# The low parts of all weights on VectorE, in a two-layer attention trunk

## The chip, the cores and the metric

One core of a Trainium2 chip runs the kernel. The metric is the device time of one execution in microseconds (us), as the median of several runs.

## The reference

The input x has 256 tokens of 1024 features. Two layers follow each other, each with a residual: `x = x + mixer(rms_norm(x))`.

```
layer 0 (nsa):  q, kc, vc, ks, vs, kw, vw, gl, z = split(h @ a_w_in)   # 1024 x 3632
                three causal attentions of 16 heads over 4 key groups:
                compressed keys, selected blocks, window; each with a gate sigmoid(gl)
                y = (gated sum of the three * silu(z)) @ a_w_out        # 1024 x 1024
layer 1 (swa):  q, k, v, z = split(h @ b_w_in)                          # 1024 x 2304
                attention in a window of 128 tokens, 2 key groups, a sink in the softmax
                y = (o * silu(z)) @ b_w_out                             # 1024 x 1024
```

Queries and most keys are normed per head and rotated before they meet. All is float32, and the comparison needs nearly all of its digits.

## The kernel before, in words

[...] To keep the digits, each operand a is split into a rounded part hi(a) and the rest lo(a) = a - hi(a), and a product is the sum hi*hi + hi*lo + lo*hi. So each weight matrix is brought in as tiles of 128 rows by 1024 numbers (two row blocks of 512 columns, four of 256 or eight of 128; three loads are narrower), 63 loads in all, and each tile goes through three steps: a DMA from the queue of SP writes `wraw`, a copy makes the rounded part `wh` (nearly always on ScalarE, L140; a few on VectorE, L142), and a subtraction makes the low part `wl = wraw - wh` (L168 where it is VectorE's, L65 where it is GpSimd's). `wraw`, `wh` and `wl` have five buffers each, so a tile's parts can be made only when TensorE is through with the tile five loads ahead.

Which engine makes a low part is read from the table `WPS` (L38): nine strings, one for each phase of the program (`PHASES`, bounds in loads), and within a phase the letters are taken in turn. `d` is VectorE, `p` is GpSimd, `b` gives the first half of the row blocks to VectorE and the second half to GpSimd. The first load is split in steps of one row block.

The program writes its steps in this order, and a scheduler of the framework, with a timeline of its own, then decides the order of the instructions on every engine; each engine runs its list strictly in order. Layer 0: transposed tokens hT, key and value products (akc, avw, akw, aks), the key preparation (`k_prep`), the compressing network (ph), query products of two groups of eight heads (aq) with `q_prep`, then gates (pz, `z_gate`) and attention (`attend0`: scores s, softmax p, transposes ptp, value products po) for four groups of heads, and the output product (pya, pyb). Layer 1 has the same steps with other names (aqb, akv, sb, pb).

Around the change it is three helpers that matter. `q_prep` and `k_prep` take the products of both halves of the tokens: a sum of squares per head (L307 on ScalarE, L308 on VectorE), the two rotary terms `rt` (L320, L321, VectorE), the reciprocal root `rsqrt` (L244 to L250: one scaling, two integer steps, and three Newton rounds of three small steps each, all on VectorE, on 128 rows of 2 to 16 numbers, in tiles rs_m, rs_t, rs_y), then on GpSimd the addition of the rotary terms and the scaling by the root (both L65, tile `rt`), the rounded part on ScalarE, the low part on VectorE (L260 into `qs`, L373 into `kp`), and transposes of both on TensorE (L347 `ptq`, L376 `ptk`), whose results the scores need. `z_gate` reads a gate's product on VectorE (L391). GpSimd also scales the softmax weights p by their sums (L70).

Of the kernel before, what the change touches and what calls it, by code (L numbers as in the profile page):

```python
"""Two-layer trunk of a hybrid decoder: a sparse-attention mixer, then a sliding-window mixer with sinks.

The sequence has 256 tokens, so the shapes alone decide that the selected branch of the first mixer takes
all four key blocks (NSA_TOPK >= n_blk) and that its window covers every earlier token: both are causal
attention over their own keys and values, and the block scores order a set that is taken whole.

Products run on the tensor engine in float32r passes. An operand a is split exactly into hi(a) + lo(a),
each of 12 mantissa bits, and hi*hi + hi*lo + lo*hi is accumulated in float32.  Queries are stacked as
[hi; lo] against [hi; hi] and [lo; lo] keys, so two passes carry all four products.
"""  # L10
# [19 lines left out]
T = 256  # L30
# [3 lines left out]
EPS = 1e-6  # L34
NEG = -1e30
HP, HPZ, HPS, HPT, HPQ, HPF = 200, 200, 0, 100, 0, 0
RSC, QLO = 'p', 'd'
WPS = ('pbdb', 'bd', 'dppd', 'bd', 'bp', 'p', 'pdp', 'ppd', 'b')  # L38
PHASES = (4, 13, 23, 29, 37, 43, 49, 55)
# [18 lines left out]
class Pool:  # L58
    """GpSimd, with steps by scalars in their two-operation form (a factor of one): its cores run that faster."""

# [18 lines left out]
def swap_halves(ap, n):  # L79
    """[128, n, 64] read with the two 32-wide halves of each head exchanged, as [128, n, 2, 32]."""  # L80
    p, h, d = ap.ap
    return bass.AP(tensor=ap.tensor, offset=ap.offset + 32, ap=[list(p), list(h), [-32, 2], [1, 32]])
# [7 lines left out]
def tile_hybrid_trunk(ctx: ExitStack, tc: tile.TileContext, x, positions, norm_gains, a_w_in, a_cmp_pos,  # L90
# [23 lines left out]

# [1 line left out]
    warm = work.tile([128, 256], BF, name="warm", tag="sq", bufs=1)  # L116
    nc.gpsimd.memset(warm, 0.0)

    def warm_up(n):
        """Products of zeros that keep the tensor engine at its full clock until the first data is there."""  # L120
        pw = bank("pw", "acc")
        for i in range(n):
            mm(pw[:, 0:256], warm[:, 0:128], warm, True, True)
# [6 lines left out]

# [1 line left out]
    nload, NLOW = [0], 4  # L132
# [65 lines left out]
    warm_up(NWARM)  # L198
# [1 line left out]
    ident0 = work.tile([128, 128], F32, name="ident0", tag="rt1")  # L200
# [7 lines left out]
    nc.vector.tensor_copy(gT, pg)  # L208
    # masks to add: [window edge | causal | zero | causal], and those of the compressed keys
    mask = const.tile([128, 512], F32, name="mask")  # L210
# [25 lines left out]

# [1 line left out]
    def rsqrt(dst, src, a, b):  # L238
        """dst = (a * src + b) ** -0.5 by a bit-level guess and three Newton steps."""
        shape = list(src.shape)  # L240
        m = work.tile(shape, F32, name="rs_m", tag="rs_m")
# [10 lines left out]
    def row_rsqrt(dst, s0, s1, a):  # L252
        """dst = (a * (s0 + s1) + EPS) ** -0.5."""
        ss = work.tile(list(dst.shape), F32, name="rs_h", tag="rs_h")
        nc.vector.tensor_tensor(ss, s0, s1, op=ALU.add)
        rsqrt(dst, ss, a, EPS)
# [7 lines left out]
    def norm_transpose(xt, layer, hT, h, ns=(0, 1)):  # L264
        """hT[:, part, k, tokens of half h] = parts of the gain-weighted rows, features on the partitions.

        The norm's factor of each row is left out here; it goes into what is made of the products."""
        for n in ns:
# [14 lines left out]
    def spread(r):  # L283
        """The row factors [tokens, 2] as rows of all partitions, [128, 256]."""
        rows = work.tile([128, T], F32, name="rrows", tag="rrows", bufs=1)
        ones = work.tile([128, 128], F32, name="ones", tag="rt2")
        nc.vector.memset(ones, 1.0)
        pr = ps_t.tile([128, T], F32, name="pr", tag="pt")
        for h in range(2):
            dg = work.tile([128, 128], F32, name="dg", tag="rt1")  # L290
            nc.vector.tensor_scalar(dg, ident, r[:, h:h + 1], None, op0=ALU.mult)
            mm(pr[:, h * 128:(h + 1) * 128], ones, dg, True, True)
        nc.scalar.activation(rows, pr, AF.Copy)
        return rows

    def proj(acc, hT, h, w, nk, k0):
        """acc[tokens of half h, columns] += h @ w over the nk row blocks from k0."""
        wh, wl = w
# [11 lines left out]
    def rope_terms(ps, n, h, tab, eng='d'):  # L310
        """The two terms of the rotated, gain-weighted heads (before the row factor)."""
        t1 = work.tile([128, n, HD], F32, name="rt1", tag="rt1")
# [17 lines left out]
    def q_prep(pss, tab, qTs, h0, rf):  # L330
        """Eight heads of both halves: norm, rotate, split, and stack [hi; lo], head dims on the partitions."""
        ssq = work.tile([128, 2, 8], F32, name="qssq", tag="qssq")
# [17 lines left out]
    def k_prep(pss, ng, tab, kt, c0, rf):  # L350
        """Key heads of both halves: norm, rotate, split, duplicate, transpose into kt[:, part, group, c0[h]:]."""
        ssq = work.tile([128, 2, ng], F32, name="kssq", tag="kssq")
# [26 lines left out]
    def z_gate(hT, wd, c0, zt, g, rows):  # L379
        """zt[:, 2 * g:2 * g + 2, :] = 2 * silu(z) of two column blocks, columns on the partitions."""  # L380
        pz = ps_a.tile([128, 2, T], F32, name="pz", tag="pz")
# [20 lines left out]
    def scores(p, s, mk, floor, nm, total):  # L402
        """p = exp(s + mask - m) with m the larger of the row's maximum and -floor; nm = -m, total = row sum of p."""
        nc.vector.tensor_tensor_reduce(out=p, in0=s, in1=mk, scale=-1.0, scalar=floor, op0=ALU.add, op1=ALU.min,  # L404
# [3 lines left out]
    def finish_unit(po, zt, h, g4, oz):  # L408
        """Gate the four heads 4*g4.. and split them for the output product."""
        if g4 == 3 and h == 1 and 1:  # L410
# [12 lines left out]
    def pv(po, blocks, first):  # L423
        """po += V^T P^T over blocks of (v [keys, 64], four P^T blocks [keys, 4, 128])."""
        for i, (v, ptb) in enumerate(blocks):
# [4 lines left out]
    def transpose_p(srcs):  # L430
        """P^T [keys, 4, 128] from four [128 queries, 128 keys] blocks."""
        pt = ps_t.tile([128, 4, 128], F32, name="ptp", tag="pt")
# [8 lines left out]
    def out_proj(oz, w, xt, sq_out, last):  # L441
        """xt += oz^T w per half; order of row blocks so that half 0 ends early."""
        ws = {}
# [7 lines left out]
        for kk, n, h in order:  # L451
# [9 lines left out]
            if last and h == 1 and n == 1:  # L461
                # the last quarter of the columns has a bank of its own
                for q in range(2):
# [16 lines left out]

    # ================= layer 0 =================
    hT = work.tile([128, 2, 8, T], F32R, name="hT", tag="hT", bufs=1)
# [23 lines left out]

# [1 line left out]
    sinks = const.tile([128, NH], F32, name="sinks")  # L508
# [7 lines left out]
    def rope_tables(cp):  # L516
        """Rows of [-sin, sin, cos] of the angles; the first layer's carry the norm's factor of the row too."""
        trig = cp.tile([128, 2, 3, 32], F32, name="trig")
# [48 lines left out]
    with tc.tile_pool(name="cmp", bufs=1) as cp:  # L567
        w2 = cp.tile([128, HD], F32, name="w2")
        posr = cp.tile([16, 2, 128], F32, name="posr", tag="hr")

        # compressed branch: keys and values of all tokens, two neighbours stacked on the partitions
        ktv = [cp.tile([128, 5, 272], F32, name=f"ktv{i}") for i in range(2)]
# [38 lines left out]
        def keys_selected():  # L611
            # keys and values of the selected and window branches, and the branch gates
            acc = banks("aks", "s")
# [29 lines left out]
        def compress():  # L643
            # the two small networks of the compressed branch
            ph = bank("ph")[:, 0:80].rearrange("p (g c) -> p g c", c=16)
# [12 lines left out]
            nc.vector.scalar_tensor_tensor(hx, hs, 1.0, hx, op0=ALU.add, op1=ALU.mult)  # L658
            # keys
            pk = bank("pk")[0:64, 0:HD]  # L660
# [16 lines left out]
            for part in range(2):  # L677
                nc.vector.tensor_copy(kt[:, part, :, 128:144], pt[:, part].rearrange("p (g c) -> p g c", c=16))
            # values
            hr = cp.tile([128, 4, 4, 16], F32, name="hr", tag="kd")  # L680
# [20 lines left out]
    def attend0(g):  # L701
        for h in range(2):
# [6 lines left out]
            for i in range(4):  # L709
# [21 lines left out]
                for m in range(2):  # L731
                    pm = p[:, m, 0] if h == 0 else p[:, m]
                    scores(pm, svs[m], mks[m], 3e38, nm[:, i, m:m + 1], sums[:, i, m + 1:m + 2])
            # compressed keys, four heads together
            cm = att.tile([128, 4], F32, name="cm", tag="cm")
# [31 lines left out]

    # ================= layer 1 =================
    sqs = work.tile([128, 2, 2], F32, name="sqs1", tag="sqs")
# [113 lines left out]
```

## Time and profile before

| | us |
|---|---|
| median of 3 runs | 316.99 |
| lowest and highest run | 315.06, 317.51 |
| span of the profiled execution | 315.0 |

| engine | busy us | share of the span |
|---|---|---|
| PE (TensorE) | 284.8 | 90% |
| DVE (VectorE) | 238.7 | 76% |
| POOL (GpSimd) | 193.6 | 61% |
| ACT (ScalarE) | 185.9 | 59% |

The profile is of one execution, whose own time outside the span is not listed; the three runs lie 0.03 to 2.5 us above its span. Times in a timeline count from the span's start. An engine's idle time before an instruction is put down to what released it. Where two engines use one resource, the profile shows no wait: an instruction that is held is merely longer.

### The profile page before, as it was taken

How to read it: one execution, taken by the hardware profiler on the slowest of the kernel's cores; microseconds unless marked ns; L12 is line 12 of the kernel's file. 1: busy time of each engine (PE TensorE's matmuls, PEld its weight loads, DVE VectorE, ACT ScalarE, POOL GpSimd, SP SyncE). 2: the span in 40 equal slices, each digit the busy share in tenths (PEclk: the TensorE clock that was granted, in tenths of full speed). 3: DMA queues.
4: the chain of work that ended last, by engine and by line, in shares of the span. 5: the costliest groups of instructions: out<-in, count | busy, mean ns of one | idle time of the engine just before them, and what ended most of it. 6: DMA issues, size and time to landing. Idle time of an engine off the chain costs nothing.

```text
span 315.0 us, 5443 instructions
## 1 busy us (share of the span) xinstructions
PE 284.8 (90%) x1772; PEld 234.5 (74%) x1772; DVE 238.7 (76%) x691; ACT 185.9 (59%) x441; POOL 193.6 (61%) x214
## 2 busy tenths in 40 slices
PE   6979999849999768979999999999929889999995
PEld 4758998637988667856767676889828888787774
DVE  2898359977999996698785433899995999987533
ACT  5674892443435764878888455555228656996610
POOL 6899637951835685563745464539777869583600
PEclk9979999978999995999999999999987979999999
DMA  7969725642454524220020526136724631200003
GB/s 223 319 206 295 286 71 133 208 127 72 128 136 142 182 79 133 69 69 0 2 68 11 193 71 197 21 113 185 211 73 149 198 122 69 67 3 0 1 2 133
DMA packets 33116, 37.53 MB, mean 119 GB/s; under 512 B 1680, under 2 KB 21568, under 8 KB 32960
## 3 DMA queue, kind: packets, MB, share of 16 engines
q1 hardware_dynamic: 33088, 37.18, 38.2%
q8 instruction: 14, 0.23, 0.3%
q14 instruction: 14, 0.11, 0.1%
HBM read 36.13 MB, written 1.05 MB: 118 GB/s over the span
## 4 chain that ended last, share of the span: by engine, by line
PE 40%; DVE 33%; issue 10%; POOL 8%; ACT 3%; DMA 3%; SPq 0%; POOLq 0%; DVEq 0%; ACTq 0%
PE po L113 6%; PE pya L113 6%; PE pz L113 6%; POOL wl L65 5%; PE ptp L434 4%; DVE wl L168 4%; DVE rs_t L248 4%; PE s L113 3%; PE pyb L113 2%; PE akc L113 2%; DVE rs_y L246 2%; PE avw L113 2%; PE aq L113 2%; DMA wraw<-in_a_w_in_dram 2%; DVE rs_m L244 2%
## 5 line engine op out<-in xcount | busy, mean ns | idle before, releaser
L65 POOL TENSOR_TENSOR wl<-wraw,wh 128x1024 fp32r<-128x1024 f32 (+3 forms) x48 | 95.5, 1998 | 33.2 <-ACT wh L140 28.9
L140 ACT ACTIVATE wh<-wraw 128x1024 fp32r<-128x1024 f32 (+3 forms) x58 | 59.3, 1031 | 18.2 <-PE pya L113 3.5
L113 PE MATMUL pz<-hT,wh 128*128 128x256 f32 x256 | 51.4, 296 | 3.3 <-DVE zt L391 3.3
L168 DVE TENSOR_TENSOR wl<-wraw,wh 128x512 fp32r<-128x512 f32 (+3 forms) x38 | 42.1, 1108 | 13.3 <-ACT wh L140 13.2
L113 PEld LDWEIGHTS pz<-hT,wh 128*128 128x128 f32 x256 | 42.5, 201 | 4.5 <-DVE zt L391 3.9
L113 PE MATMUL pz<-hT,wl 128*128 128x256 f32 x128 | 37.8, 295 | 0.0
L70 POOL TENSOR_SCALAR p<-p,rg 128x256 f32<-128x256 f32 (+1 forms) x48 | 21.9, 478 | 21.7 <-DVE rg L742 17.8
L406 ACT ACTIVATE p<-p,nm 128x128 f32<-128x128 f32 (+1 forms) x64 | 28.5, 448 | 6.7 <-DVE nm L404 6.3
L140 ACT ACTIVATE ptsb<-ptp 128x512 f32<-128x512 f32 x36 | 20.8, 591 | 12.0 <-PE ptp L434 11.9
L65 POOL TENSOR_TENSOR rt<-rt,rt 128x512 f32<-128x512 f32 (+2 forms) x14 | 16.4, 1175 | 16.9 <-DVE rt L321 13.0
L404 DVE CUSTOM_DVE_ANT_0 p<-s,mask 128x128 f32<-128x128 f32 (+1 forms) x64 | 21.1, 347 | 6.5 <-PE s L113 5.9
L113 PEld LDWEIGHTS pz<-hT,wl 128*128 128x128 f32 x128 | 25.6, 200 | 0.1
L113 PE MATMUL s<-kt,qT 128*128 128x272 f32 (+1 forms) x96 | 21.7, 318 | 2.4 <-DVE nm L404 2.4
L113 PE MATMUL aqb<-wh,hT 128*128 128x512 f32 x64 | 22.0, 416 | 0.0
L113 PE MATMUL aq<-wh,hT 128*128 128x512 f32 x64 | 21.5, 408 | 0.0
L113 PEld LDWEIGHTS s<-kt,qT 128*128 128x128 f32 x96 | 14.9, 192 | 7.4 <-issue 2.1
L70 POOL TENSOR_SCALAR pb<-pb,rg 128x128 f32<-128x128 f32 (+1 forms) x24 | 11.7, 504 | 11.6 <-DVE rg L838 4.5
L406 ACT ACTIVATE pb<-pb,nm 128x128 f32<-128x128 f32 (+1 forms) x32 | 14.2, 445 | 5.4 <-DVE nm L404 5.1
L347 PE MATMUL ptq<-identr,qs 128*128 128x128 f32 x64 | 8.2, 272 | 9.2 <-DVE qs L260 8.9
L434 PE MATMUL ptp<-identr,p 128*128 128x128 f32 x96 | 15.9, 279 | 0.0
L113 PE MATMUL po<-ptsb,vv 128*64 128x256 f32 x96 | 15.4, 403 | 0.0
L347 PEld LDWEIGHTS ptq<-identr,qs 128*128 128x128 f32 x64 | 7.2, 154 | 10.9 <-DVE qs L260 9.5
(248 smaller groups left out, 762.4 us busy)
## 6 DMA issues: line engine op xcount, KB each, us to landing
wraw<-in_a_w_in_dram SPq DMA_DIRECT2D x25, 512.0 KB, 3.9
wraw<-in_b_w_in_dram SPq DMA_DIRECT2D x18, 512.0 KB, 3.9
wraw<-in_a_w_out_dram SPq DMA_DIRECT2D x8, 512.0 KB, 3.8
wraw<-in_b_w_out_dram SPq DMA_DIRECT2D x8, 512.0 KB, 4.0
x<-in_x_dram SPq DMA_DIRECT2D x4, 256.0 KB, 4.2
w<-in_cmp_w_dram SPq DMA_DIRECT2D x1, 1024.0 KB, 5.3
x<-in_x_dram SPq DMA_DIRECT2D x2, 512.0 KB, 3.7
wraw<-in_a_w_in_dram SPq DMA_DIRECT2D x2, 456.0 KB, 3.8
```

What stands on the lines that cost most here:

```text
L65: self.eng.tensor_tensor(out, a, b, op=op)
L70: self.eng.tensor_scalar(out, a, s0, s1, op0=op0, op1=op1)
L113: nc.tensor.matmul(o, lhsT=l, rhs=r, start=start, stop=stop)
L140: nc.scalar.activation(dst, src, AF.Copy)
L168: e_.tensor_tensor(wl[:, ks], raw[:, ks], wh[:, ks].bitcast(F32), op=ALU.subtract)
L244: nc.vector.tensor_scalar(m, src, a, b, op0=ALU.mult, op1=ALU.add)
L246: nc.vector.tensor_scalar(y.bitcast(I32), t.bitcast(I32), -1.0, 1597463007.0, op0=ALU.mult, op1=ALU.add)
L248: nc.vector.tensor_tensor(t, y, y, op=ALU.mult)
L347: nc.tensor.transpose(pt[:, i], qs[:, 4 * b + i].rearrange("p a d -> p (a d)"), identr)
L404: nc.vector.tensor_tensor_reduce(out=p, in0=s, in1=mk, scale=-1.0, scalar=floor, op0=ALU.add, op1=ALU.min, accum_out=nm)
L406: nc.scalar.activation(p, p, AF.Exp, scale=-1.0, bias=nm, accum_out=total)
L434: nc.tensor.transpose(pt[:, i], s, ident)
```

## The change

The table `WPS` gives every low part to VectorE. Since all letters are `d`, a tile's low part is one instruction, and of the first load, which goes in steps, two. Nothing else of the program differs: the rest of the difference takes out comments and docstrings line by line, so that the line numbers stay.

```diff
-WPS = ('pbdb', 'bd', 'dppd', 'bd', 'bp', 'p', 'pdp', 'ppd', 'b')
+WPS = ('d', 'd', 'd', 'd', 'd', 'd', 'd', 'd', 'd')
```

The scheduler then writes other orders on every engine. First place, TensorE, where the second group of queries of layer 0 is transposed (ptq); before:

```order
L113 MATMUL pz<-hT,wl 128x256
L113 MATMUL s_1311<-kt,qT_192 128x256 x2
L347 MATMUL ptq<-identr,qs 128x128 x8
L113 MATMUL s_1319<-kt,qT_192 128x272 x2
L347 MATMUL ptq<-identr,qs 128x128 x4
L113 MATMUL pz<-hT,wh 128x256 x2
```

And now, where pz is a gate's product and s a score's:

```order
L113 MATMUL pz<-hT,wl 128x256
L113 MATMUL s_1221<-kt,qT_191 128x272 x2
L113 MATMUL s_1230<-kt,qT_191 128x272 x2
L347 MATMUL ptq<-identr,qs 128x128 x8
L113 MATMUL s_1288<-kt,qT_192 128x272 x2
L113 MATMUL s_1292<-kt,qT_192 128x256 x2
L347 MATMUL ptq<-identr,qs 128x128 x8
L113 MATMUL s_1300<-kt,qT_192 128x272 x2
```

Before, 48 of the 192 products pz of layer 0 stand behind this ptq; now the last of them stands ahead of it, and eight more of the score products stand behind it. VectorE's list has 23 instructions for low parts ahead of the second qs that this ptq reads before, and 35 now.

Second place, TensorE in layer 1, the first ptq there, between the products of the second query group (aqb); before:

```order
L113 MATMUL aqb_2897<-wh,hT_2374 128x512 x2
L113 MATMUL aqb_2897<-wl,hT_2374 128x512
L113 MATMUL aqb_2897<-wh,hT_2374 128x512
L347 MATMUL ptq<-identr,qs 128x128 x8
L113 MATMUL aqb_2898<-wh,hT_2374 128x512
```

And now:

```order
L113 MATMUL aqb_2884<-wl,hT_2360 128x512
L113 MATMUL aqb_2884<-wh,hT_2360 128x512
L113 MATMUL pz<-hT_2360,wh 128x256 x2
L113 MATMUL pz<-hT_2360,wl 128x256
...
L347 MATMUL ptq<-identr,qs 128x128 x8
L113 MATMUL pz<-hT_2360,wl 128x256
```

Before, 30 of the 48 products aqb of the second group stand ahead of the ptq and 18 behind it; now all 48 and 11 products of the second gate stand ahead.

Third place, VectorE in layer 1, where the reciprocal roots of the first query group (128x16) begin; before:

```order
L244 TENSOR_SCALAR rs_m<-qssq 128x16
L168 TENSOR_TENSOR wl<-wraw,wh 128x1024
L245 TENSOR_SCALAR rs_t<-rs_m 128x16
L308 TENSOR_REDUCE kssq<-sq 128x2
L246 TENSOR_SCALAR rs_y<-rs_t 128x16
L248 TENSOR_TENSOR rs_t<-rs_y 128x16
L249 SCALAR_TENSOR_TENSOR rs_t<-rs_t,rs_m 128x16
```

And now:

```order
L168 TENSOR_TENSOR wl<-wraw,wh 128x1024 x2
L244 TENSOR_SCALAR rs_m<-qssq 128x16
L308 TENSOR_REDUCE kssq<-sq 128x2
L168 TENSOR_TENSOR wl<-wraw,wh 128x1024
L245 TENSOR_SCALAR rs_t<-rs_m 128x16
L168 TENSOR_TENSOR wl<-wraw,wh 128x1024
L308 TENSOR_REDUCE kssq<-sq 128x2
L246 TENSOR_SCALAR rs_y<-rs_t 128x16
L391 TENSOR_TENSOR zt_2449<-pz,rrows 128x512
```

The low parts that stood in GpSimd's list now stand between the small steps: from layer 1's first residual addition (L477) to the second qs there are 13 in VectorE's list, where there were 3.

## Rows read from the trace of the kernel before

**Rows 1.** The page: span; engine, busy us, share of the span, instructions.

```profile
span 315.0 us, 5443 instructions
PE 284.8 (90%) x1772; PEld 234.5 (74%) x1772; DVE 238.7 (76%) x691; ACT 185.9 (59%) x441; POOL 193.6 (61%) x214
```

**Rows 2.** Timeline of PE: start, duration, instruction, in brackets the idle time before it.

```profile
68.23 0.72 PE L376 MATMUL ptk<-identr,kp 128*128 128x128 f32 x4 [4.26 <-POOL rt L65]
...
118.81 1.25 PE L347 MATMUL ptq<-identr,qs 128*128 128x128 f32 x8 [3.40 <-DVE qs L260]
...
235.71 1.26 PE L347 MATMUL ptq<-identr,qs 128*128 128x128 f32 x8 [5.53 <-DVE qs L260]
...
253.41 0.50 PE L113 MATMUL pz<-hT,wh 128*128 128x256 f32 x2 [2.02 <-DVE zt L391]
```

**Rows 3.** A stretch: length, busy PE, PEld, DVE, ACT, POOL (instructions), granted clock, DMA share, GB/s.

```profile
66.70:73.50 6.80, 5.27 (x36) 4.53 (x37) 4.58 (x14) 4.18 (x8) 3.51 (x5) 0.50 0.55 148
```

**Rows 4.** Groups by form: count, busy us, mean ns, idle before.

```profile
L65 POOL TENSOR_TENSOR wl<-wraw,wh 128x1024 fp32r<-128x1024 f32 x24 | 59.0, 2468 | 10.7 <-ACT wh L140 10.7
L65 POOL TENSOR_TENSOR wl<-wraw,wh 128x512 fp32r<-128x512 f32 x22 | 34.1, 1552 | 22.5 <-ACT wh L140 18.2 <-DVE wh L142 2.4 <-DMA wraw<-in_a_w_in_dram 1.9
L168 DVE TENSOR_TENSOR wl<-wraw,wh 128x1024 fp32r<-128x1024 f32 x15 | 22.3, 1489 | 4.3 <-ACT wh L140 4.3
```

**Rows 5.** Timeline of DVE in 217 to 236 us.

```profile
219.47 1.21 DVE L168 TENSOR_TENSOR wl<-wraw,wh 128x1024 fp32r<-128x1024 f32 x1
...
223.16 2.32 DVE L248 TENSOR_TENSOR rs_t<-rs_y 128x16 f32<-128x16 f32 x1
225.52 0.18 DVE L249 SCALAR_TENSOR_TENSOR rs_t<-rs_t,rs_m 128x16 f32<-128x16 f32 x1
...
228.48 0.97 DVE L249 SCALAR_TENSOR_TENSOR rs_t<-rs_t,rs_m 128x4 f32<-128x4 f32 x1
...
231.80 2.26 DVE L248 TENSOR_TENSOR rs_t<-rs_y 128x4 f32<-128x4 f32 x1
```

**Rows 6.** Timeline of POOL in 217 to 236 us.

```profile
223.04 2.41 POOL L65 TENSOR_TENSOR wl<-wraw,wh 128x1024 fp32r<-128x1024 f32 x1
227.37 2.06 POOL L65 TENSOR_TENSOR rt<-rt,qr 128x512 f32<-128x512 f32 x2 [1.92 <-DVE rs_t L249]
229.39 4.65 POOL L65 TENSOR_TENSOR wl<-wraw,wh 128x1024 fp32r<-128x1024 f32 x2
```

**Rows 7.** Timeline of DVE in 45 to 119 us: first and last of eight held steps.

```profile
46.78 2.36 DVE L244 TENSOR_SCALAR rs_m<-kssq 128x8 f32<-128x8 f32 x1
...
109.39 2.05 DVE L248 TENSOR_TENSOR rs_t<-rs_y 128x16 f32<-128x16 f32 x1
```

**Rows 8.** Tile wl alone: stage, length, busy PE, PEld, DVE, POOL, clock, DMA.

```profile
0.00:45.00 45.00, 19.35 (x54) 11.22 (x54) 10.92 (x12) 11.73 (x9) 0.96 0.75 245
45.00:119.00 74.00, 30.81 (x90) 17.36 (x90) 12.61 (x12) 24.25 (x12) 0.95 0.44 128
119.00:193.00 74.00, 15.16 (x42) 8.52 (x42) 2.16 (x3) 20.77 (x10) 0.96 0.25 77
193.00:236.00 43.00, 21.63 (x65) 12.15 (x64) 4.50 (x2) 19.95 (x8) 0.98 0.44 126
```

**Rows 9.** Busy time of all instructions by stage (columns as in Rows 3).

```profile
0.00:45.00 45.00, 40.22 (x214) 34.06 (x215) 27.98 (x70) 29.77 (x51) 32.62 (x57) 0.96 0.75 245
45.00:119.00 74.00, 62.83 (x415) 53.85 (x413) 68.45 (x164) 35.42 (x70) 48.20 (x38) 0.95 0.44 128
119.00:193.00 74.00, 71.41 (x446) 52.94 (x446) 46.08 (x217) 53.70 (x160) 42.53 (x56) 0.96 0.25 77
193.00:236.00 43.00, 37.48 (x224) 32.32 (x223) 39.27 (x83) 19.27 (x34) 26.97 (x16) 0.98 0.44 126
```

**Rows 10.** The chain of waits in 262 to 268 us: start, duration, piece.

```profile
264.19 2.89 PE pz L113 x22
```

**Rows 11.** Waits: who waited for whom, us in total, times, longest.

```profile
DVE wl L168 <- ACT wh L140: 13.2, 12, 2.6
```

## The prediction

> **What bounds the kernel now.** I read the page's busy shares first, then TensorE's waits in order of time, then the two vector engines beside each other in the stages around those waits. TensorE is busy 284.8 of 315.0 us; VectorE 238.7 and GpSimd 193.6 [rows 1]. So the time is TensorE's work plus what it stands still. It stands longest at four places: 4.26 us at 64 us, 3.40 at 115, 5.53 at 230 and 2.02 at 251 [rows 2], 15.2 us in all, and each time a chain of small steps on VectorE, or a row scaling on GpSimd that waits for one, ends last. [...]
>
> The chains are long because VectorE is held. A low part of 128x1024 on GpSimd takes 2468 ns, on VectorE 1489 [rows 4]. What the reader is to see in [rows 5, 6] is what the two cost each other: from 229.39 us GpSimd has two low parts, 4.65 us, and in that time VectorE's step on 128x4 numbers at 231.80 takes 2.26 us and ends with the second of them. The same kind of step takes 0.18 us at 225.52, when GpSimd is idle. At 223.16 it is 2.32 us beside one low part of 2.41 us.
>
> **The change, part by part.** It does what it says: the built order has no low part on GpSimd and 64 instructions for it on VectorE (38 now, the halves of a shared tile becoming one).
>
> *What is added to VectorE.* Undisturbed, a 128x1024 costs it 1.21 us [rows 5]; of 128x512 I take half of that and a little, 0.69 us. GpSimd's 48 pieces are 24 of 1024 and 22 of 512 numbers a row [rows 4] and two narrower ones, together some 36 tiles of 1024: 36 x 1.21 = 43.6 us more. GpSimd loses 24 x 2.468 + 22 x 1.552 + 2.6 for the two = 95.9 us.
>
> *What VectorE gets back.* In 45 to 119 us eight of its steps are held by a low part of GpSimd, the first at 46.78 us (2.36 us for 128x8), the last at 109.39 us (2.05 us) [rows 7]; against 0.18 us each, or 1.21 for a low part of its own, they lose 12.5 us. GpSimd's low parts there fill 24.25 us [rows 8]: 7 of 1024 and 4 of 512 and the start of a twelfth, which cost VectorE 7 x 1.21 + 4 x 0.69 = 11.2 us. In 193 to 236 us six held steps lose 12.2 us ([rows 5] has two of them), and 8 pieces of 1024 (19.95 us on GpSimd) come to 9.7 us. So in both stages in which VectorE is nearly full (68.45 of 74 us, 39.27 of 43 [rows 9]) its load stays what it is, within 3 us. In the other stages it has room, and those pieces are hidden: 46.08 busy of 74 us between 119 and 193 us [rows 9]. If that cover were gone, the 20.77 us of GpSimd there would come to 20.77 x 1.21 / 2.47 = 10.2 us.
>
> *What is moved in the order.* The scheduler puts more of TensorE's work ahead of the transposes it waits for. First place, second query group: all 192 products of the gates (pz) stand ahead of the waiting ptq, where 48 stood behind it; 8 score products stand behind that were ahead. From 22 pz in 2.89 us [rows 10], 0.131 us each: 48 x 0.131 = 6.3 us, less 8 x 0.14 = 1.1: 5.2 us of the stop is filled, if VectorE comes to its second qs when it does now. Does it? By then it has done 35 low parts, not 23: 35 x 1.21 less 1.6 for the narrower ones is 40.7 us, 17.2 more than the 10.92 + 12.61 now spent [rows 8]. Of these, half of GpSimd's 11.73 us ahead of 45 us (5.9) falls where VectorE is idle 17 us [rows 9]; 12.5 us and some 2.5 of the first stage come back. Each low part of VectorE now waits 13.2 / 38 = 0.35 us on average for ScalarE's rounded part [rows 11], and behind it waits all of VectorE's queue; 12 more make 4.2. 17.2 - 5.9 - 15 + 4.2 = +0.5 us. Term: -4.7 us.
>
> Second place, layer 1: 18 more products of aqb and 11 of pz stand ahead of the ptq that waits 5.53 us. 11 x 0.131 = 1.4; an aqb has twice the columns, so 18 x 0.26 = 4.7: 6.1 us. VectorE's load there is even, but ten more low parts stand ahead of qs and wait 0.35 each: +3.5. Term: -2.6 us.
>
> Against it, the 48 pz are missing where they stood, beside the first softmax groups. TensorE is busy 71.41 of 74 us there [rows 9]; without filler it can stand still between 0 and 6.3 us more. No row lies near either end: VectorE, on which the scores wait, has 28 us of room in that stage, but the first groups now start just behind its full stage. I take half, +3 us.
>
> The sum is -4.7 - 2.6 + 3 = -4.3 us: the span goes from 315.0 to 310.7. The median of the runs shown, 316.99, lies 1.96 us above the profiled span (the runs go from 315.06 to 317.51), and I carry that over: **312.7 us**. The first term lies between -11 (GpSimd's row scalings, no longer behind 2.4 us pieces, bring qs 6 us earlier) and +3 (half the relief fails); the second between -5.5 and +3.5; the third between 0 and +6.3. [...]
>
> The row shows that the hold lasts until GpSimd's piece ends. [...]
>
> **The rivals.**
> 1. *VectorE becomes the bound (slower).* It is in order: a low part whose rounded part or buffer isn't there stops the reciprocal roots, scores and splits behind it. For it: in two stages it is over 90% busy, and GpSimd's row scalings, which stay, also hold it (0.97 us at 228.48 beside the scalings from 227.37 [rows 5, 6]). If half the relief fails, the first term is -4.7 + 7.5 = +2.8, the second -2.6 + 6.1 = +3.5, with +3 from the third: +9.3, or **326 us**. It decides when more than 4.3 of the 27.2 us of both reliefs fails, a sixth. Against it: the holds are seen to end with GpSimd's low parts. Chance 0.34. [...]
> 2. *The stops only move (no change).* TensorE's work is the same, and the missing filler costs its full 6.3 us: -4.7 - 2.6 + 6.3 = -1.0, **316 us**. For it: the softmax groups hang on VectorE and ScalarE both. Against it: VectorE's room in that stage [rows 9]. Chance 0.24.
> 3. *The stops vanish (much faster).* All 15.2 us go but 5, and half of what a slow stretch costs (1.7) with them: 317.0 - 11.9 = **305 us**. For it: every one of them ends on a held chain. Against it: the pieces come into the same queue. Chance 0.08.
>
> The forecast has 0.34. A measurement of this kernel tells 1% from no change, 3.2 us: faster means below 313.8, slower above 320.2. Faster is the forecast and rival 3, 0.42; within 1% 0.24; slower 0.34. The likeliest case's own range is 308 to 316; the range that reaches over most of the others is 304 to 326.
>
> **What would show it.** In the profile after: no low part on GpSimd, and its busy time near 193.6 - 95.9 = 98 us; VectorE between 240 and 262 us; its small steps of the roots at 0.2 us, hardly any above 1; low parts of 128x1024 at 1.2 us. TensorE's stop before the second ptq under 2 us, and that of layer 1 under 3. If VectorE's waits for ScalarE's rounded parts grow well past 25 us, or TensorE stands before the first softmax groups for more than 6 us, rival 1 or 2 has it. The forecast is wrong if the small steps stay long without GpSimd's low parts, for then something else holds them.

## The result, and the profile after

The changed kernel takes 304.44 us (median of four runs, 303.87 to 306.27) against 316.13 us (four runs, 315.06 to 317.51): a ratio of 0.9637, 95% interval 0.959 to 0.9685. It is 3.6% faster, where 1.4% was forecast, and 304.44 is just inside the range.

First the page of the kernel after, as [rows 1]: span; then engine, busy us, share, instructions.

```profile
span 302.5 us, 5413 instructions
PE 284.7 (94%) x1772; PEld 232.3 (77%) x1772; DVE 231.9 (77%) x717; ACT 186.1 (62%) x441; POOL 110.2 (36%) x166
```

TensorE's work is the same to 0.1 us. What is gone is its standing still: the idle times in its timeline add up to 26.6 us before and to 14.2 after, 12.4 of the 12.5 us that the span lost. VectorE has 26 low parts more and is busy 6.8 us less.

The timeline of PE after, its transposes and longest stops, in answer to [rows 2] (start, duration, instruction, idle time before it):

```profile
69.50 0.54 PE L376 MATMUL ptk<-identr,kp 128*128 128x128 f32 x4
...
103.89 0.88 PE L347 MATMUL ptq<-identr,qs 128*128 128x128 f32 x8 [1.83 <-DVE qs L260]
...
114.63 0.89 PE L347 MATMUL ptq<-identr,qs 128*128 128x128 f32 x8 [0.32 <-DVE qs L260]
...
119.03 0.76 PE L113 MATMUL s<-kt,qT 128*128 128x272 f32 x4 [1.25 <-DVE nm L404]
...
229.66 0.80 PE L347 MATMUL ptq<-identr,qs 128*128 128x128 f32 x8
...
237.92 0.50 PE L113 MATMUL pz<-hT,wh 128*128 128x256 f32 x2 [1.95 <-DVE zt L391]
```

The 4.26 us at the ptk (the fourth group of four, now at 69.50) and the 5.53 us at layer 1's ptq have gone altogether. The ptq that waited 3.40 us, that of the second query group, waits 0.32 (at 114.63). A new stop of 1.83 us stands ahead of the first group's ptq (at 103.89), which waited for nothing before. The pz stop stayed (2.02, now 1.95).

Two stretches after (length, busy PE, PEld, DVE, ACT, POOL with instructions, granted clock, DMA share, GB/s), the first over the place of [rows 3], the second beside the first softmax groups:

```profile
60.00:89.00 29.00, 29.00 (x216) 24.63 (x215) 22.63 (x49) 15.19 (x27) 12.88 (x12) 1.00 0.49 133
...
120.00:130.50 10.50, 9.74 (x38) 7.38 (x40) 6.91 (x48) 7.71 (x31) 3.49 (x9) 0.51 0.13 46
```

In the first TensorE never stands (busy 29.00 of 29.00 us) and its granted clock is 1.00. In the second the granted clock is 0.51: of 10.5 us some 5.1 are lost, by an estimate from that clock, behind the stops at 114 to 119 us.

Groups by form after, as [rows 4] (count, busy us, mean ns, idle before):

```profile
L168 DVE TENSOR_TENSOR wl<-wraw,wh 128x1024 fp32r<-128x1024 f32 x59 | 77.1, 1312 | 17.8 <-ACT wh L140 17.5
...
L65 POOL TENSOR_TENSOR rt<-rt,rt 128x512 f32<-128x512 f32 x8 | 13.8, 1728 | 16.8 <-DVE qr L250 6.1 <-PE akv L113 4.6 <-DVE rt L321 4.5
...
L248 DVE TENSOR_TENSOR rs_t<-rs_y 128x16 f32<-128x16 f32 x12 | 2.6, 217 | 0.1
...
L244 DVE TENSOR_SCALAR rs_m<-qssq 128x16 f32<-128x16 f32 x4 | 0.7, 170 | 0.0
```

The same forms before, which [rows 4] did not show:

```profile
L65 POOL TENSOR_TENSOR rt<-rt,rt 128x512 f32<-128x512 f32 x8 | 12.2, 1535 | 10.3 <-DVE rt L321 8.5 <-DVE rs_t L245 1.4 <-DVE rs_m L244 0.5
...
L248 DVE TENSOR_TENSOR rs_t<-rs_y 128x16 f32<-128x16 f32 x12 | 6.6, 548 | 0.2
...
L244 DVE TENSOR_SCALAR rs_m<-qssq 128x16 f32<-128x16 f32 x4 | 4.4, 1106 | 0.0
```

The small steps have their short time back, most of them (1106 to 170 ns, 548 to 217), and GpSimd's row additions are longer (1535 to 1728 ns). VectorE's timeline after, in 210 to 230 us, answers to [rows 5]: between low parts the small steps take 0.16 us, and the one of 1.00 us stands beside GpSimd's row scalings.

```profile
218.25 0.16 DVE L246 TENSOR_SCALAR rs_y<-rs_t 128x16 int32<-128x16 int32 x1
...
219.08 1.21 DVE L168 TENSOR_TENSOR wl<-wraw,wh 128x1024 fp32r<-128x1024 f32 x1
220.22 0.16 DVE L245 TENSOR_SCALAR rs_t<-rs_m 128x4 int32<-128x4 int32 x1
...
225.82 1.00 DVE L250 SCALAR_TENSOR_TENSOR kr<-rs_t,rs_y 128x4 f32<-128x4 f32 x1
```

### The profile page after: what moved, and what is told of

Same layout as the page of the kernel before. It is cut to its first block, busy times and chain, and to the rows that moved or that the text cites. A ratio compares the mean times of both kernels' runs of the same rounds, so it can differ in the third digit from the quotient of the medians.

```text
span 302.5 us, 5413 instructions
## 1 busy us (share of the span) xinstructions
PE 284.7 (94%) x1772; PEld 232.3 (77%) x1772; DVE 231.9 (77%) x717; ACT 186.1 (62%) x441; POOL 110.2 (36%) x166
## 4 chain that ended last, share of the span: by engine, by line
PE 74%; DVE 15%; issue 3%; POOL 2%; DMA 2%; ACT 2%; SPq 1%; ACTq 0%; DVEq 0%
PE po L113 9%; PE pz L113 8%; PE pya L113 8%; PE aq L113 7%; PE pyb L113 7%; PE ptp L434 6%; PE aqb L113 5%; DVE wl L168 5%; PE s L113 5%; PE aks L113 4%; PE avw L113 2%; DMA posi<-in_positions_dram 2%; PE akw L113 2%; PE akv L113 2%; PE ph L113 2%
## 5 line engine op out<-in xcount | busy, mean ns | idle before, releaser
L168 DVE TENSOR_TENSOR wl<-wraw,wh 128x1024 fp32r<-128x1024 f32 (+2 forms) x64 | 81.9, 1285 | 19.1 <-ACT wh L140 18.8
L113 PE MATMUL pz<-hT,wh 128*128 128x256 f32 x256 | 50.4, 294 | 2.8 <-DVE zt L391 1.9
L113 PEld LDWEIGHTS pz<-hT,wh 128*128 128x128 f32 x256 | 42.1, 199 | 3.5 <-DVE zt L391 2.1
L65 POOL TENSOR_TENSOR rt<-rt,rt 128x512 f32<-128x512 f32 (+2 forms) x14 | 22.2, 1588 | 30.1 <-DVE rt L321 16.6
L113 PEld LDWEIGHTS s<-kt,qT 128*128 128x128 f32 x96 | 16.5, 216 | 6.9 <-issue 3.1
L113 PE MATMUL aqb<-wh,hT 128*128 128x512 f32 x64 | 20.6, 394 | 0.0
L113 PE MATMUL aq<-wh,hT 128*128 128x512 f32 x64 | 20.5, 394 | 0.0
L434 PE MATMUL ptp<-identr,p 128*128 128x128 f32 x96 | 16.9, 291 | 0.0
L404 DVE CUSTOM_DVE_ANT_0 pb<-sb,mask,nsink 128x128 f32<-128x128 f32 (+1 forms) x32 | 11.8, 411 | 5.4 <-PE ptp L434 4.0
L434 PEld LDWEIGHTS ptp<-identr,p 128*128 128x128 f32 x96 | 11.7, 147 | 3.9 <-issue 1.8
L65 POOL TENSOR_TENSOR rt<-rt,qr 128x512 f32<-128x512 f32 x8 | 10.2, 1295 | 11.9 <-DVE rs_t L248 9.3
L406 ACT ACTIVATE pb<-pb,nm 128x128 f32<-128x128 f32 (+1 forms) x32 | 14.2, 444 | 0.6 <-DVE nm L404 0.6
```

What stands on the lines that cost most here:

```text
L65: self.eng.tensor_tensor(out, a, b, op=op)
L113: nc.tensor.matmul(o, lhsT=l, rhs=r, start=start, stop=stop)
L168: e_.tensor_tensor(wl[:, ks], raw[:, ks], wh[:, ks].bitcast(F32), op=ALU.subtract)
L406: nc.scalar.activation(p, p, AF.Exp, scale=-1.0, bias=nm, accum_out=total)
L434: nc.tensor.transpose(pt[:, i], s, ident)
```

## Experiments

Two things changed at once: the place of the low parts, and with it the order that the scheduler gives TensorE. TensorE's traced instructions are the same 1643 in both kernels, so either order can be laid on either kernel by edges that fix the order of issue alone.

For each kernel two starts on TensorE serve as milestones: that of the last product of layer 0's output (pyb), and that of the last product of all (tail). Here are the two of the kernel after, from its timeline; before they stand at 199.59 and 311.22 us.

```profile
194.51 0.39 PE L113 MATMUL pyb<-wh,oz 128*128 128x512 f32 x1
...
299.05 0.28 PE L113 MATMUL tail<-wh,ozb 128*128 128x256 f32 x1
```

The first milestone is called layer 0 below, the difference of the two layer 1. Each comes from one profiled execution, so a difference under 1 us says little.

| kernel | low parts | order | time, us | ratio (95%) | layer 0 | layer 1 |
|---|---|---|---|---|---|---|
| before | shared | old | 316.1 | 1 | 199.59 | 111.63 |
| x1 | VectorE | old | 311.7 | 0.9843 (0.9797-0.989) | 199.03 | 106.01 |
| x2 | shared | new | 321.9 | 1.0147 (1.0101-1.0192) | 201.16 | 117.31 |
| after | VectorE | new | 304.4 | 0.9637 (0.959-0.9685) | 194.51 | 104.54 |
| x9 | VectorE | old, then new | 309.7 | 0.9814 (0.9735-0.9893) | 199.28 | 105.23 |
| x10 | VectorE | new, then old | 307.0 | 0.9693 (0.9612-0.9773) | 195.65 | 106.59 |

### Place and order apart: x1 and x2

```diff
+ORDER = {'EngineType.PE': '0-21 30 36 31-33 37-39 ...'}   # x1: the order of before
+def pin_order(nc, tc):
+    ...
+        for a, b in zip(idx, idx[1:]):
+            tc.add_manual_dep(traced[b], traced[a].name, mybir.DependencyInfo(
+                mybir.DependencyClass.NoSync, mybir.DependencyReason.DATA), reason="order")
...
         tile_hybrid_trunk(tc, *args, out)
+        pin_order(nc, tc)
```

x1 is this on the changed kernel. 

> All low parts on VectorE, but TensorE's instructions in exactly the order of the kernel before (issue order alone; ScalarE's follows to within a place or so). Theory A (the holds: VectorE's small steps no longer wait for GpSimd's low parts): the gain stays, 302 to 308 us, and TensorE's stop at the first ptk, 4.26 us before, is below 1. Theory B (the new order of TensorE's work fills the stops): the gain goes, 313 to 318 us. Theory C (GpSimd's row additions and scalings no longer queue behind its low parts): as A.

x2 is the kernel before with the order of after. 

> The low parts shared as before, TensorE's instructions in exactly the order of the changed kernel. Theory B: 303 to 308 us, the stops filled. Theories A and C: 312 to 322 us, with the stops at ptk and ptq still 3 us and longer; work put ahead of a late ptq can win at most what my prediction gave it, 7 us.

x1 lies between the ranges of A and B. x2 lies just inside A's (321.9 us), but its stops at the ptk and at layer 1's ptq are 2.65, 1.85 and 2.38 us, under the 3 that A gave them, and TensorE stands ahead of gate products instead. So neither theory holds alone: the new place alone gains 1.6%, the new order alone loses 1.5%, and together they gain 3.6%. The order pays only with the new place. The stops of x1, as [rows 2]:

```profile
60.35 0.75 PE L376 MATMUL ptk<-identr,kp 128*128 128x128 f32 x4 [2.47 <-ACT kp L367]
...
67.92 0.54 PE L376 MATMUL ptk<-identr,kp 128*128 128x128 f32 x4
...
119.97 0.37 PE L347 MATMUL ptq<-identr,qs 128*128 128x128 f32 x1 [4.51 <-DVE qs L260]
...
232.19 0.88 PE L347 MATMUL ptq<-identr,qs 128*128 128x128 f32 x8 [2.58 <-DVE qs L260]
```

In the old order the second ptq waits longer than before (4.51 against 3.40), layer 1's ptq half as long (2.58 against 5.53). The ptk that waited 4.26 us waits for nothing in x1 (at 67.92), but now the first of the four groups waits 2.47, at 60.35, where it waited 0.54. So place alone gave layer 0 nothing (199.03 against 199.59) and layer 1 5.6 us. The stage of the ptk, 40 to 100 us, in before, x1 and after (length, busy PE, PEld, DVE, ACT, POOL with instructions, granted clock, DMA share, GB/s):

```profile
40.00:100.00 60.00, 54.01 (x343) 45.56 (x340) 51.53 (x106) 27.23 (x46) 34.61 (x25) 0.94 0.45 126
```

```profile
40.00:100.00 60.00, 53.67 (x332) 44.95 (x331) 47.90 (x114) 28.76 (x48) 18.01 (x17) 0.92 0.51 141
```

```profile
40.00:100.00 60.00, 59.12 (x404) 51.78 (x402) 48.61 (x113) 29.91 (x46) 19.20 (x18) 1.00 0.55 158
```

TensorE stands still for 6.0 us of them before, 6.3 in x1 and 0.9 after: here the new place alone only moves the stops, and the order on top of it fills them. The two longest stops in x2:

```profile
107.05 0.76 PE L113 MATMUL pz<-hT,wh 128*128 128x256 f32 x2 [5.72 <-DVE rs_t L249]
...
256.47 0.79 PE L113 MATMUL pz<-hT,wh 128*128 128x256 f32 x2 [4.99 <-DVE zt L391]
```

With GpSimd's low parts still there, gate products that were put ahead wait 5 us for VectorE in both layers: the new order runs TensorE close behind VectorE's list. In the changed kernel the nearest such stops are 0.88 us (at 95.31) and 1.95.

### Which layer: x8, x9, x10

x8 takes the change in layer 0 alone.

```diff
-WPS = ('pbdb', 'bd', 'dppd', 'bd', 'bp', 'p', 'pdp', 'ppd', 'b')
+WPS = ('d', 'd', 'd', 'd', 'd', 'p', 'pdp', 'ppd', 'b')
```

> Low parts all on VectorE in layer 0 (loads 0 to 36), shared as before in layer 1. In the trace of the changed kernel the end of layer 0's output product comes 5.1 us earlier, that of the kernel 12.5. If the two layers' gains add, 310 to 313 us; if layer 0's gain is lost again, 315 to 318 us.

311.8 us, ratio 0.9866 (0.9796 to 0.9936); layer 0 at 194.88, layer 1 111.56 long. The gains of the layers add, and neither is lost again.

x9 and x10 lay the old order on one layer of the changed kernel (the list of x1 cut at its 993rd instruction, the end of layer 0's output product; the other layer keeps the new order).

```diff
+        idx = [i for i in idx if i < 993]   # x9; x10: i >= 993
```

> All low parts on VectorE; TensorE's instructions in the order of the kernel before up to the end of layer 0's output product, in the order of the changed kernel from there. With the old order throughout the time was 311.7 us, with the new one 304.4. Theory D (layer 0's order carries the difference, mostly the products put ahead of the ptk and beside the gates, which my prediction gave no term): 309 to 312 us. Theory E (my terms: the first place with its missing filler is worth 1.7 us, the second 2.6): 305 to 307 us.

> As the last, the other way round: the order of the changed kernel in layer 0, that of the kernel before in layer 1. Theory D: 304 to 306 us. Theory E: 306 to 308 us, with 1 to 3 us of stop at layer 1's first ptq.

In the new place the order is worth 4.8 us in layer 0 (199.28 against 194.51) and 2.1 in layer 1 (106.59 against 104.54). x9's time is in theory D's range, x10's in E's: D holds for the larger part, and layer 1's part is near the forecast's term.

### The place of the second ptq: x13

The 48 products of layer 0's last gate go back behind the ptq of the second query group; all else is the changed kernel. The place in TensorE's list:

```diff
-s x4, pz x16, ptq x4, pz x32, s x4, ptq x8, s x4, ptq x8, s x16, ptcs, ptp x4
+s x4, ptq x4, s x4, ptq x8, s x4, ptq x4, pz x19, ptq x4, s x12, pz x6, s x4, ptcs, pz x14, ptp x4, pz x9
```

> The changed kernel with its own order on TensorE but for the 48 products of layer 0's last gate (pz), which stand where they stood before the change: behind the second group's first ptq and beside the first softmax groups. My prediction's first and third terms together (-4.7 + 3) make their new place worth 1.7 us: then 305 to 307 us. If their absence beside the softmax groups costs more than they fill (7.3 us of stop and half clock are lost there in the trace of the changed kernel), 299 to 303 us.

305.57 us, ratio 0.9654 (0.9609 to 0.9699); layer 0 ends at 195.39, 0.9 us later than after. Its stops there:

```profile
109.73 1.29 PE L113 MATMUL s<-kt,qT 128*128 128x272 f32 x4 [2.40 <-DVE nm L404]
...
112.42 1.25 PE L347 MATMUL ptq<-identr,qs 128*128 128x128 f32 x8 [1.40 <-DVE qs L260]
```

The two more stops take what the filler gives back behind them. The net of the first and third term, 1.7 us, is compatible with that, and so is nothing at all, since the interval overlaps that of the changed kernel. That the missing filler costs more than its products fill (299 to 303 us) is not.

### Hold or queue: x3 to x6, x14

That VectorE is held is read in the timeline; but GpSimd's own row steps also queued behind its low parts, and the change frees both. x3, x4 and x5 put work back on GpSimd in the changed kernel, in its fixed order, for the old share of tiles (the pattern is the old WPS). The line of x3, x4 and x5:

```diff
+scr = wpool.tile(list(raw.shape), BF, name="scr", tag="scr", bufs=1)
+pool.tensor_tensor(scr[:, ks], raw[:, ks], wh[:, ks].bitcast(F32), op=ALU.subtract)          # x3
+pool.tensor_scalar(scr[:, ks], wh[:, ks].bitcast(F32), 1.0, 1.0, op0=ALU.mult, op1=ALU.mult)  # x4, twice
+pool.memset(scr[:, ks], 0.0)                   # x5, three times, behind a scaling of 128x16 of wh
```

> The changed kernel with its order on TensorE fixed; GpSimd in addition does the subtraction of its old share of tiles into a scratch tile (bf16) that nobody reads, so its load and its two-input steps are back and nothing waits for their result. Theory A: the small steps of the roots are again 1 to 2.4 us beside them, VectorE's load grows by 20 to 35 us, and the time is 314 to 328 us. Theory B: 303 to 306 us. Theory C: 310 to 317 us.

> As the kernel with the extra subtractions, but each is replaced by two GpSimd steps that scale the rounded part by one (one input, the same scratch tile), near 1.05 us each for 128x1024 by the step of that size in the trace of before, so about 70 to 85 us of GpSimd's time are filled. In the trace of before, steps with one input on GpSimd hardly lengthen VectorE's. Theory A: 303 to 308 us, small steps at 0.2 us. Theory C: GpSimd's row steps queue behind them as before the change, 310 to 317 us. Theory B: 303 to 306 us.

> As the kernel with one-input extras, but each extra is three GpSimd steps that only write (memsets of the scratch tile) behind a scaling of 128x16. GpSimd's queue is filled again; the extras read next to nothing. Theory A (holds), if a memset holds nobody: small steps at 0.2 us and 303 to 309 us. Theory C (GpSimd's own row steps queue behind such pieces): 310 to 325 us even with small steps at 0.2 us. If memsets hold VectorE as well, the small steps show it and the run tells nothing between A and C.

They took 350.8, 332.5 and 323.4 us (ratios 1.1091, 1.0487, 1.0257). x3 is longer than any theory had it: VectorE, with all low parts and the holds, is busy 283.9 us, 52 more than in the changed kernel. x4 and x5 were meant as controls that hold nobody, and are not. From x5: the group of the memsets, VectorE's steps with one input in 209 to 213 us, the memsets of that time, and a product with two inputs beside other memsets (L253, L254 and L257 are L244, L245 and L248 of before):

```profile
L74 POOL MEMSET scr<- 128x1024 bf16 x72 | 69.8, 970 | 3.0
...
209.59 0.95 DVE L253 TENSOR_SCALAR rs_m<-rs_h 128x2 f32<-128x2 f32 x1
...
210.57 0.97 DVE L254 TENSOR_SCALAR rs_t<-rs_m 128x2 int32<-128x2 int32 x1
...
209.56 2.97 POOL L74 MEMSET scr<- 128x1024 bf16 x3
...
231.12 0.18 DVE L257 TENSOR_TENSOR rs_t<-rs_y 128x16 f32<-128x16 f32 x1
...
230.10 2.97 POOL L74 MEMSET scr<- 128x1024 bf16 x3
```

Beside memsets, whose mean is 0.97 us, these two steps with one input took 0.95 and 0.97 us, the product with two inputs 0.18. So x5 alone tells nothing between A and C, as its expectation allowed. The three together tell something. TensorE's order is the same in them, and GpSimd's queue does not get shorter from one to the next (it is busy 214.3, 222.3 and 231.8 us), while VectorE's busy time falls (283.9, 263.4 and 237.1 us) and the time falls by 27 us. So work on GpSimd that holds VectorE more costs more, though its queue is no longer. On the other side, x5 takes 19 us more than the changed kernel with VectorE busy only 5 us more. That points at the queue, but does not show it, since the memsets' holds lie on the same chains.

x6 and x14 go the other way: the shared low parts stay, and GpSimd's row steps move to VectorE; in x14 TensorE has the old order in addition.

```diff
-RSC, QLO = 'p', 'd'
+RSC, QLO = 'd', 'd'
-RSK, KLO = 'p', 'dp'
+RSK, KLO = 'd', 'dp'
-OZL, RTE, SSE = 'd', 'p', 'd'
+OZL, RTE, SSE = 'd', 'd', 'd'
```

> The kernel before, low parts shared as before, but the row additions and row scalings of queries and keys on VectorE instead of GpSimd, so that nothing on the way to a transpose queues behind GpSimd's low parts. Theory C: 305 to 312 us. Theory A: the holds stay (small steps to 2.3 us) and VectorE gets about 15 us more to do: 313 to 322 us.

> The kernel before, low parts shared as before, row additions and scalings of queries and keys on VectorE, TensorE's instructions exactly in the old order. Layer 1 (from the end of layer 0's output product to the last product) takes 111.5 us in the trace of before and 105.9 with the low parts on VectorE in the same order. Theory C (queue): 105 to 108. Theory A (holds): 110 to 113, with steps of 2.3 us still there. Whole time: C 309 to 313, A 314 to 318 us.

x6: 312.6 us, ratio 0.9897 (0.9853 to 0.994), between the two theories. x14: 322.5 us, ratio 1.0158 (1.0099 to 1.0217); layer 1 takes 115.97 us, 4.3 more than before. Theory A had that direction, though not the size, and the holds go on in x14. From the timelines of VectorE and TensorE there:

```profile
225.87 2.32 DVE L246 TENSOR_SCALAR rs_y<-rs_t 128x16 int32<-128x16 int32 x1
...
232.74 2.36 DVE L249 SCALAR_TENSOR_TENSOR rs_t<-rs_t,rs_m 128x4 f32<-128x4 f32 x1
...
232.87 0.88 PE L347 MATMUL ptq<-identr,qs 128*128 128x128 f32 x8 [1.02 <-DVE qs L260]
```

But at layer 1's first ptq x14 gains more than x1: the stop of 5.53 us is 1.02 there and 2.58 in x1, and from the second sum of squares to qs VectorE takes 14.47 us (217.66 to 232.13), against 18.97 before and 15.45 in x1. What x14 loses stands behind it, at a ptk (2.18 us), a pz (2.53) and a ptp that waits for a scaling on GpSimd (3.26). Its row steps are also shorter, and VectorE's own list differs. So how x1's gain is shared between the end of the holds and the shorter queue stays open: no run takes the holds away and leaves GpSimd's load.

### Further on VectorE: x7, x12, x11, x15

x7 makes the edit of x6 in the changed kernel. x12 makes it for RSC and RSK alone. x11 is x7 with one scaling more on VectorE.

```diff
-PSL = 'pppd'
+PSL = 'dpdd'   # x11
```

> The changed kernel with the row additions and scalings on VectorE too. They are the two-input steps on GpSimd that still hold VectorE (8 to 9 of the 15 us that its steps lose there beside their undisturbed time), and each is near 1 us shorter on VectorE. Theory A: the time falls on, to 297 to 303 us. Rival (VectorE becomes the bound, 232 us busy and some 15 more): 306 to 312 us.

> The changed kernel with the row scalings alone on VectorE, the row additions still on GpSimd. Theory A: half of the remaining holds by GpSimd's row steps go (3.9 us of VectorE's excess is beside the scalings), 301 to 305 us. If the time is set by TensorE's work and what stops remain elsewhere, 304 to 306 us.

> The changed kernel with the row additions and scalings on VectorE and, in layer 1, one of GpSimd's three scalings of probabilities of a head group (of four) moved to VectorE as well (two on each). TensorE's longest stop in the kernel with the rows on VectorE, 3.58 us at 255.85 us, waits for such a scaling on GpSimd. If that stop goes with its slow stretch of 1.7 us, 300 to 303 us; if another step ends last there, 304 to 307.

305.3, 305.6 and 307.0 us (ratios 0.9679, 0.9674, 0.9722): none is told apart from the changed kernel to its good. In x11 the stop that was to go stayed: 3.51 us, now for the scaling on VectorE. The milestones gave a hint: x7 ends layer 0 at 192.80, 1.7 us earlier than after, and loses that in layer 1 (107.10).

x15 takes the row steps to VectorE in layer 0 alone, with the changed kernel's order of layer 1.

```diff
+            rte = 'd' if tab < 4 else 'p'
-            ENG[RTE].tensor_tensor(t1, t1, t2, op=ALU.add)
+            ENG[rte].tensor_tensor(t1, t1, t2, op=ALU.add)
...   # the scaling behind it likewise, and both in k_prep
```

> All low parts on VectorE; row additions and scalings on VectorE in layer 0, on GpSimd in layer 1; TensorE in layer 1 in the changed kernel's order. With the rows on VectorE throughout, layer 0 ended at 193.2 us (changed kernel 194.9) and layer 1 took 107.0 us (104.4). If these add up: 301.5 to 303.5 us. If not: 304 to 306.

303.4 us, ratio 0.9576 (0.9543 to 0.9609), the lowest; layer 0 at 192.72, layer 1 105.00. The parts add up as expected. Its interval overlaps that of the changed kernel, so that it beats it is not shown.

## Why the prediction was wrong, point by point

The direction was right, and the mechanism in part: the small steps are short again, and work put ahead fills stops. The size was not: the span lost 12.5 us, of which 5.1 in layer 0 (forecast 1.7) and 7.1 in layer 1 (forecast 2.6). What came out is near rival 3's 305 us, which had 0.08.

*The step that failed first: "4.26 us at 64 us" got no term.* The prediction read that stop in [rows 2], and its slow stretch stands in [rows 3] with a clock of 0.50, but it costed the order at two places only. The new order puts ahead of that ptk all 48 products of the first query group (25 stood there) and 35 gate products, and in 40 to 100 us TensorE now stands 0.9 us in place of 6.0, at a clock of 1.00 in place of 0.94. It takes both halves of the change: in x1 another 6.3 us are lost there, in x2 the products put ahead wait. Layer 0's order is worth 4.5 us (x1 against after, 199.03 to 194.51); x13 puts the place of the second ptq at 0.9 of it. By difference some 3.6 us fell where the sum had nothing; no run changes the order of this stage alone.

*The second: in layer 1, "ten more low parts ... wait 0.35 each: +3.5".* Two tiles of that stretch, from layer 0's end to the first ptq, in before and then in x1, which has the same order on TensorE: low parts (wl), then the steps that read or write rs_t (columns: busy time per engine that has any, then clock, DMA share, GB/s).

```profile
200.00:237.00 37.00, 18.74 (x57) 10.94 (x58) 4.50 (x2) 19.95 (x8) 0.96 0.44 128
...
200.00:237.00 37.00, 14.92 (x33) 0.96 0.44 128
```

```profile
199.40:234.00 34.60, 19.23 (x59) 11.21 (x59) 14.69 (x12) 1.00 0.62 175
...
199.40:234.00 34.60, 6.05 (x33) 1.00 0.62 175
```

VectorE gets 10.2 us of low parts (forecast 9.7) and gets back 8.9 us on 33 small steps alone. But it waits there for rounded parts only 0.5 us (0.3 before), not 3.5 more. An average over the whole program was laid on a stretch that has none of those waits. From the second sum of squares to qs it takes 15.45 us (216.01 to 231.46) where it took 18.97 (216.00 to 234.97). So the place alone gave layer 1 5.6 us, where the term's own part had a loss (how much of it is the holds, how much GpSimd's queue, x14 leaves open); and with the stop at 2.58 us, 6.1 us of products ahead could win little more: 1.5 to 2.1 us.

*The clock.* The forecast's sum has no term for it. Rival 3's sum has 1.7 us for half of a slow stretch, a term that no run shows: by an estimate from the granted clock of half-microsecond stretches, 3.4, 3.4, 3.4 and 1.7 us were lost behind the four stops before, and after, the stretches behind the ptk and layer 1's ptq are gone whole. In all the clock cost layer 0 the same before and after (8.5 us each), layer 1 5.1 us before and 1.7 after. x1 has no slow stretch there, with a stop of 2.58 us left:

```profile
226.00:260.00 34.00, 30.29 (x224) 27.73 (x223) 31.43 (x90) 24.48 (x61) 15.84 (x17) 1.00 0.47 149
```

Before, 226 to 260 us had a clock of 0.85. The stops got more than shorter: of the four, two went with their slow stretches and a third went to 0.32 us. In layer 0 new slow stretches, at 106 and 120 us, cost 1.7 and 5.1 us, as much as those behind the ptk and the second ptq had.

*First and third term.* -4.7 + 3 = -1.7; x13 says 0.9 to 1.1 for the two together, and no run measures them apart. The first was too large as it stood: it puts 5.2 us of work into a stop of 3.40 us, which can give back no more than itself. The stop lost 3.1 us. That VectorE would come to the second qs 0.5 us later was near: in x1, with the old order, that ptq waits 1.1 us longer. The missing filler shows in the changed kernel as the stop of 1.25 us and the stretch at 0.51 above.

*The load.* 36 tiles of 1024 at 1.21 us were to add 43.6 us; low parts took 42.1 us before and take 81.9 now. VectorE's total was forecast at 240 to 262 us and is 231.9, since all its other work fell from 196.6 to 150.0 us. That is 46.6 us of relief; the two stages that were counted had 24.7 in their held steps, and the others were given none but 2.5 in the first.

*GpSimd.* 110.2 us, not 98: what stays on it got 12 us longer (1535 to 1728 ns for a row addition). The sum had no term for that. On the way to the two transposes it came to 1.0 us: the two scalings ahead of layer 1's first ptq take 3.03 us, beside a low part that itself takes 1.70 in place of 1.21, where they took 2.06, and those ahead of the second ptq took 1.04 each both times.

```profile
223.78 3.03 POOL L65 TENSOR_TENSOR rt<-rt,qr 128x512 f32<-128x512 f32 x2 [9.34 <-DVE rs_t L248]
...
224.20 1.70 DVE L168 TENSOR_TENSOR wl<-wraw,wh 128x1024 fp32r<-128x1024 f32 x1 [0.30 <-ACT wh L140]
```

*The signs.* Small steps at 0.2 us, low parts at 1.2 to 1.3, the stop before the second ptq under 2 us and layer 1's under 3, waits for rounded parts under 25 us: all came. VectorE's and GpSimd's busy time did not, as said. The waits:

```profile
DVE wl L168 <- ACT wh L140: 18.8, 18, 4.2
```

*Rival 1* had 0.34 and found nothing: VectorE is not the bound. The busier vector engine took 40 us of low parts more and is busy less, 231.9 us in place of 238.7, for its busy time was in part time in which it was held. *Rival 2* saw that the missing filler costs, and lost to the stage at 64 us and to layer 1's shorter chain, which the sum gave nothing or a loss.

## What to carry to other kernels

Where two engines hold each other, as here, busy time is not load (VectorE took 39.8 us more of low parts and was busy 6.8 us less): take the held part of it off before judging whether an engine has room for more work. When a change lets a scheduler reorder, cost every long stop of the bounding engine against the new order, not the two where the difference is easiest to see. A wait averaged over a program is no price for a stretch; read the stretch.

## What the runs showed of the hardware

- In x5 GpSimd steps that only write held VectorE's steps with one input, even small ones: beside memsets (970 ns on average), steps on 128x2 numbers took 0.95 to 0.97 us (from 209.59 us), where 0.15 to 0.16 is their time with GpSimd idle (before, from 205.52 us). A product with two inputs of 128x16 took 0.18 us beside memsets (at 231.12 us). Over the whole of x5 the step with one input on 128x16 integers (L254) averages 932 ns, that product (L257) 273.
- In x4 GpSimd steps with one input of 128x1024 (1348 ns on average) held VectorE's small steps: one on 128x8 integers took 1.02 us (from 61.23 us), where its mean in the changed kernel is 0.16.
- The granted clock did not follow the length of a stop: behind the 1.83 us at 103.89 in the changed kernel 106 to 110 us had a granted clock of 0.57 (0.50 in most of it), behind 2.58 us in x1's layer 1 it stayed at 1.00. What decides it no run here shows.
